# Second attention of a two-block network: float32 value products on the array's column halves, sums on GpSimd

## Chip, cores and metric

One core of one Trainium2 chip. The metric is the device time of one execution in microseconds. Of three runs of the kernel before, the median is 4474.56 us (4474.19 to 4477.1).

## What is computed

Two blocks of a network over 2048 tokens of width 1024, all in float32: block 1 (latent attention, a state space part), block 2 (attention and retention side by side, then routed experts). The change lies in block 2's attention: eight query heads, two key/value heads, 2304 keys (256 of a context and 2048 tokens), head width 64.

```python
def _attend(q, k, v):
    qb = jnp.moveaxis(q.reshape(B, nb, Q_BLOCK, ATTN_KV_HEADS, GQA_GROUP, HEAD_DIM), 1, 0)
    scale = HEAD_DIM ** -0.5
    def one_block(q_blk):
        s = jnp.einsum('bqhgd,bkhd->bhgqk', q_blk, k).astype(jnp.float32) * scale
        p = jax.nn.softmax(s, axis=-1)
        return jnp.einsum('bhgqk,bkhd->bqhgd', p.astype(v.dtype), v)
```

## The kernel before

`whole` runs the phases one after another. `phase_b` projects the tokens; its `do_kv` splits the values into a high and a low part (`R` is the type fp32r, `F` is float32) and stores both. `phase_attn2` (L1310) then runs `Attention2`, with `Retention.steps` in its gaps, and `phase_out2` follows.

`Attention2` works in 32 units: 128 queries of the four heads that share keys, so 512 columns (head, query). A unit goes through 18 key tiles of 128 keys. For a tile t:

- `scores` (L1176): two fp32r products of 512 columns into one PSUM bank `ps`.
- `exps` (L1185): the exponential on ScalarE (L1187) into `p`, and a rounded copy `ph` in fp32r (L1191).
- `rest` (L1193), one tile later: the remainder `pl` = p - ph (L1199), on DVE for even t and on GpSimd (POOL in the rows) for odd t, by the string `LO`. By the string `ACC` the row sums of `ph` are taken by TensorE for ten tiles ("E") and by DVE for eight ("D", L1209, tile `accD`); `fold` splits that sum at the end.
- `values` (L1223), five tiles later (`LAG`): `ph` against both parts of the values (L1232, tile `o`), `pl` against a block of 64 columns of ones beside the high part (L1234, L1238, tile `o1`), and a single row of ones against `ph` and the two parts of the sum (L1236). All are fp32r products of 512 columns, 48 in a unit.

While a unit runs, `top` (L1154) takes the next unit's maxima: 20 products into `pa` (L1161; 16 of 512 columns, four of 256), each with a maximum on DVE (L1162), out of two banks. `finish` (L1240) adds the parts, sends the sums through memory to be spread over partitions, and divides (GpSimd, L1254 and L1265).

Retention takes four steps in a unit (tiles 1, 9, 11, 15, `SIDE`). A chunk of it has six: among them four DVE steps on the state (`rst`, L1049), a power on GpSimd (`r`, L72), four DVE steps that wait for it (`on`, L1076), transposes of `on`, a product on GpSimd (`ot`, L1086), and a spread of queries on GpSimd (`qx`, L966). The last three units have none of it.

Every engine takes its instructions in the order of its own list; the framework's scheduler makes the lists from the order of the code in `run` and adds waits on semaphores.

Of the kernel before, what the change touches and what calls it, by code (L numbers as in the profile page):

```python
# [33 lines left out]
class K:  # L34
    """What every part of the kernel shares: the core, the arguments, constants, small helpers."""
# [76 lines left out]
# Chunks of 16 tokens. Lanes of the tables: (direction, state). A table of powers has 17 entries e:  # L112
# lambda^e forward, lambda^(16 - e) backward.
# [3 lines left out]
def early(k):  # L117
    """What rests on the parameters alone, in small parts."""
# [56 lines left out]
        # Powers 0..16, ascending for both directions: [lanes, e, g].  # L175
# [16 lines left out]
        # Bbar = (lambda_bar - 1) / lambda B  # L192
# [18 lines left out]
        # Tables with e in the direction's order; pw: lambda^s' forward, lambda^(15 - s') backward.  # L211
# [10 lines left out]
        # Bbar with columns (direction, h), zero off its direction.  # L222
# [869 lines left out]
class Attention2:  # L1092
# [92 lines left out]
    def exps(self, u, t):  # L1185
# [4 lines left out]
        if self.HI[t] == "A":  # L1190
            self.nc.scalar.copy(hi, p)  # L1191
# [1287 lines left out]
```

## Time and profile before

| what | value |
|---|---|
| median of three runs | 4474.56 us |
| profiled execution, span of its instructions | 4460.7 us |
| what lies around the span, against the median | 13.9 us |
| TensorE (PE), busy share of the span | 91% |
| DVE | 73% |
| ScalarE (ACT) | 52% |
| GpSimd (POOL) | 45% |

The profile gives the span of its one execution and no device time of its own for it, so the span is set against the median. Busy shares are means over phases with different limits. TensorE's is not a measure of work: its products are pipelined, and a row's duration is the time from its start to its end, which is longer than the step to the next start. In the rows an arrow stands between what is written and what is read, "idle before" is what the engine waited ahead of an instruction, and `x` is a count. A float32 product is two rows, each with half of its passes: `s5_out` asks for 64 products at its L1394 and the trace has 128.

### The profile page before, as it was taken

The numbers are of one execution on the slowest core, as the hardware profiler recorded it, in microseconds if no ns is written. First come the engines' busy times: TensorE is split into PE (matmuls) and PEld (weight loads), VectorE is DVE, ScalarE is ACT, GpSimd is POOL, SyncE is SP. The second block draws the span as 40 slices with busy tenths as digits, with TensorE's granted clock in tenths as the row PEclk, the third lists the DMA queues.
The fourth block names the chain that finished last, engine by engine and source line by source line (L and its number), as shares of the span: only waits on it lengthen the run. The fifth ranks groups of instructions, "written<-read, shape, count | busy, mean of one in ns | idle before, by whom it ended". The sixth has DMA issues, their size and how long they took to land. (4 is left out here: it accounts for less than half of the span.)

```text
span 4460.7 us, 60030 instructions
## 1 busy us (share of the span) xinstructions
PE 4063.1 (91%) x19842; PEld 3214.7 (72%) x19842; DVE 3244.0 (73%) x5326; ACT 2301.0 (52%) x4166; POOL 1988.3 (45%) x2239
## 2 busy tenths in 40 slices
PE   7999889999988989999888888989898799999997
PEld 5777768888876878887666666666587677777775
DVE  7563368887625365534999999999765778888886
ACT  3233455555524343322667777777521556666664
POOL 3430078882003422222555555555300566666664
PEclk9999989999998999999999999999999899999998
DMA  5543852331253464334421111110352788888885
GB/s 142 169 146 109 280 192 74 92 112 53 66 160 123 132 206 127 121 103 135 117 71 52 50 45 43 50 41 25 96 172 95 265 279 280 284 280 275 277 282 184
DMA packets 432999, 647.63 MB, mean 145 GB/s; under 512 B 88576, under 2 KB 228096, under 8 KB 432428
## 3 DMA queue, kind: packets, MB, share of 16 engines
q1 hardware_dynamic: 403868, 562.67, 39.9%
q0 software_dynamic: 21840, 66.25, 4.2%
q10 hardware_dynamic: 6976, 14.85, 1.0%
q8 instruction: 157, 2.57, 0.2%
q14 instruction: 158, 1.29, 0.1%
HBM read 496.33 MB, written 156.10 MB: 146 GB/s over the span
## 5 line engine op out<-in xcount | busy, mean ns | idle before, releaser
L1199 POOL TENSOR_TENSOR pl<-p,ph 128x512 fp32r<-128x512 f32 x288 | 416.1, 1450 | 244.8 <-ACT ph L1191 189.4
L2251 DVE TENSOR_TENSOR wlo<-raw,whi 128x1024 fp32r<-128x1024 f32 x256 | 471.6, 1855 | 66.1 <-ACT whi L2248 66.0
L2248 ACT CAST whi<-raw 128x1024 fp32r<-128x1024 f32 x384 | 394.9, 1048 | 130.9 <-DMA raw<-in_moe_w_up 43.9
L1162 DVE TENSOR_REDUCE nm<-pa 128x1 f32<-128x512 f32 (+1 forms) x640 | 390.0, 623 | 19.7 <-PE pa L1161 18.4
L1187 ACT ACTIVATE p<-ps 128x512 f32<-128x512 f32 x576 | 333.2, 599 | 105.6 <-PE ps L1183 87.0
L1161 PE MATMUL pa<-kk,q 128*128 128x512 f32 (+1 forms) x640 | 266.3, 425 | 95.7 <-DVE nm L1162 85.1
L1191 ACT CAST ph<-p 128x512 fp32r<-128x512 f32 x576 | 342.6, 624 | 7.7
L2251 POOL TENSOR_TENSOR wlo<-raw,whi 128x1024 fp32r<-128x1024 f32 x128 | 319.6, 2504 | 53.5 <-ACT whi L2248 47.4
L310 PE MATMUL z<-wh,hlo 128*128 128x512 f32 (+2 forms) x816 | 304.7, 374 | 0.0
L308 PE MATMUL z<-wh,hhi 128*128 128x512 f32 (+2 forms) x768 | 291.4, 381 | 7.5 <-DVE zo L455 2.4
L309 PE MATMUL z<-wl,hhi 128*128 128x512 f32 (+2 forms) x768 | 289.4, 377 | 2.7 <-DVE wl L319 2.7
L72 POOL TENSOR_TENSOR nr<-nr,mhalf 128x1 f32<-128x1 f32 x98 | 61.7, 631 | 499.2 <-DVE nr L70 441.1
L1199 DVE TENSOR_TENSOR pl<-p,ph 128x512 fp32r<-128x512 f32 x288 | 275.4, 956 | 9.8 <-ACT ph L1191 8.3
L1161 PEld LDWEIGHTS pa<-kk,q 128*128 128x128 f32 x640 | 124.0, 195 | 198.4 <-DVE nm L1162 167.0
L1182 PE MATMUL ps<-q,kk 128*128 128x512 f32 x576 | 241.5, 420 | 0.3
L661 PE MATMUL s<-kn,q 128*128 128x512 f32 x768 | 230.0, 407 | 10.0 <-ACT p L674 5.7
L1238 PE MATMUL o<-pl,v 128*128 128x512 f32 x544 | 220.4, 409 | 17.3 <-DVE pl L1199 12.6
L1232 PE MATMUL o<-ph,v 128*128 128x512 f32 x576 | 233.0, 407 | 2.7 <-DVE oc L1249 2.5
L1183 PE MATMUL ps<-qm,kl 65*128 65x512 f32 x576 | 229.0, 407 | 0.2
L1209 DVE TENSOR_TENSOR accD<-accD,ph 128x512 f32<-128x512 f32 x192 | 224.7, 1170 | 0.3
L693 ACT CAST ph<-pt 128x512 fp32r<-128x512 f32 x256 | 142.8, 596 | 151.1 <-PE pt L65 147.8
L697 DVE TENSOR_TENSOR pl<-pt,ph 128x512 fp32r<-128x512 f32 x256 | 167.9, 685 | 67.4 <-ACT ph L693 66.8
(634 smaller groups left out, 11924.5 us busy)
## 6 DMA issues: line engine op xcount, KB each, us to landing
raw<-in_moe_w_gate SPq DMA_DIRECT2D x128, 512.0 KB
raw<-in_moe_w_up SPq DMA_DIRECT2D x128, 512.0 KB
raw<-in_moe_w_down SPq DMA_DIRECT2D x128, 512.0 KB
raw<-in_w_in SPq DMA_DIRECT2D x136, 256.0 KB
w<-in_w_ada SPq DMA_DIRECT2D x96, 256.0 KB
xt<-in_x SPq DMA_DIRECT2D x32, 512.0 KB
xt<-x SPq DMA_DIRECT2D x28, 512.0 KB
rv<-rv SPq DMA_DIRECT2D x34, 256.0 KB
```

What stands on the lines that cost most here:

```text
L308: nc.tensor.matmul(out, lh, rh, start=start, stop=False)
L309: nc.tensor.matmul(out, lh, rl, start=False, stop=False)
L310: return nc.tensor.matmul(out, ll, rh, start=False, stop=stop)
L1161: nc.tensor.matmul(pa[:, :c1 - c0], q[:, h], kk[:, c0:c1], start=True, stop=True)
L1162: nc.vector.tensor_reduce(nm[:, h, c:c + 1], pa[:, :c1 - c0], axis=AX.X, op=OP.max)
L1182: nc.tensor.matmul(ps, kk[:, ts], q, start=True, stop=False)
L1187: self.nc.scalar.activation(p, u["s"].pop(t), AF.Exp, scale=self.scale)
L1191: self.nc.scalar.copy(hi, p)
L1199: (nc.vector if self.LO[t] == "D" else nc.gpsimd).tensor_tensor(lo, p, hi.bitcast(F), op=OP.subtract)
L1232: nc.tensor.matmul(u["o"], v[:, t, 64:], hi, start=first, stop=last)
L2248: nc.scalar.copy(hi, raw)
L2251: i = eng.tensor_tensor(lo, raw, hi.bitcast(F), op=OP.subtract)
```

## The change

The exponentials are no longer split: `ph`, `pl`, `fold` and the strings are gone. `p` lives in a ring of ten tiles and goes into the products in float32. The values are stored and loaded once, in float32, 64 columns to a tile.

Two key tiles are multiplied together: the even tile's values stand in columns 0 to 63 of the array and give partitions 0 to 63 of `o`, the odd tile's stand in columns 64 to 127 and give partitions 64 to 127. The 512 columns go in two halves of 256, so a pair has four float32 products (column half 0, 1, 0, 1). `finish` adds the two halves of `o` as before, without a third part.

The sums of the exponentials are 17 additions a unit on GpSimd, each onto the result of the last (`acc`), and one float32 product of `acc` with a column of ones at the unit's end. In `do_kv` a copy on ScalarE takes the place of the split.

```diff
 class Attention2:
     LAG = 5
-    RING = 8
+    RING = 10
...
-            v = cp.tile([128, self.NK, 192], R, name=f"v{g}")         # ones, high and low parts
+            v = cp.tile([128, self.NK, 64], F, name=f"v{g}")
...
-            nc.sync.dma_start(v[:, :, 64:].bitcast(F), k.v2[g].rearrange("t p n -> p t n"))
-            nc.gpsimd.tensor_copy(v[:, :, 0:64], k.ones[:, None, 0:64].to_broadcast([128, self.NK, 64]))
+            nc.sync.dma_start(v, k.v2[g].rearrange("t p n -> p t n"))
...
     def exps(self, u, t):
-        p = self.wk.tile([128, 512], F, name="p", bufs=5)
+        u["p"][t] = p = self.wk.tile([128, 512], F, name="p", bufs=self.RING)
         self.nc.scalar.activation(p, u["s"].pop(t), AF.Exp, scale=self.scale)
-        hi = self.wk.tile([128, 512], R, name="ph", bufs=self.RING)
-        u["p"][t] = [p, hi]
-        if self.HI[t] == "A":
-            self.nc.scalar.copy(hi, p)
 
     def rest(self, u, t):
+        if t:
+            acc = u["acc"] if t > 1 else self.wk.tile([128, 512], F, name="acc")
+            self.nc.gpsimd.tensor_tensor(acc, u["acc"], u["p"][t], op=OP.add)
+            u["acc"] = acc
+        else:
+            u["acc"] = u["p"][0]
...
     def values(self, u, t):
         nc = self.nc
...
+        if t % 2 == 0:
+            return
+        if t == 1:
             u["o"] = self.pO.tile([128, 512], F, name="o")
-            u["o1"] = self.pO.tile([128, 512], F, name="o1")
         v = self.kv[u["n"] % 2][2]
-        hi, lo = u["p"].pop(t)
-        nc.tensor.matmul(u["o"], v[:, t, 64:], hi, start=first, stop=last)
...
+        ps = [u["p"].pop(t - 1), u["p"].pop(t)]
+        for half in range(2):
+            cs = slice(256 * half, 256 * half + 256)
+            for i in range(2):
+                nc.tensor.matmul(u["o"][64 * i:64 * i + 64, cs], v[:, t - 1 + i], ps[i][:, cs],
+                                 start=t == 1 and half == 0, stop=t == self.NK - 1 and half == 1)
+        if t == self.NK - 1:
+            u["o1"] = self.pO.tile([1, 512], F, name="o1")
+            nc.tensor.matmul(u["o1"], self.k.ones[:, 0:1], u["acc"], start=True, stop=True)
 
     def finish(self, u):
...
-        nc.scalar.copy(s, o1[64:128])
...
-        nc.gpsimd.tensor_tensor(c, c, s, op=OP.add)
...
         def do_kv(z, s):
...
-            vt = wk.tile([128, 2, 2, 64], R, name="vt")
...
-            split(nc, vt[:, :, 0], vt[:, :, 1], v)
...
+            vt = wk.tile([128, 2, 64], F, name="vt")
+            nc.scalar.copy(vt, v)
```

TensorE's list at the end of a unit, before (`o_25496` is the unit's `o1`; `kk_20808` serves the maxima of the next unit; "waits" names the engine whose semaphore is waited for):

```order
L1161 MATMUL pa<-kk_20808,q 128x512 [waits DVE_49]
L1232 MATMUL o<-ph,v_20810 128x512
L1236 MATMUL o_25496<-ph,on_20802 1x512
L1236 MATMUL o_25496<-sumh,on_20802 1x512
L1182 MATMUL ps<-q,kk_20820 128x512 [waits Activation_49]
L1183 MATMUL ps<-qm,kl_20821 128x512
L1236 MATMUL o_25496<-suml,on_20802 1x512
L1238 MATMUL o_25496<-pl,v_20810 128x512 [waits Pool_49]
L1161 MATMUL pa<-kk_20808,q 128x256 [waits DVE_49]
```

and now (L1155 is `pa`, L1173 and L1174 are the scores, L1201 the value products, L1205 the sums, `o_27650` their tile `o1`):

```order
L1155 MATMUL pa<-kk_20788,q 128x512 [waits DVE_49]
L1173 MATMUL ps<-q,kk_20799 128x512 [waits Activation_49]
L1174 MATMUL ps<-qm,kl_20800 128x512
L1201 MATMUL o<-p,v_20790 64x256 x4
L1205 MATMUL o_27650<-acc,ones 1x512 [waits Pool_49]
L1155 MATMUL pa<-kk_20788,q 128x256 [waits DVE_49]
```

The value products stand in groups of four, and the product of the sums, which waits for GpSimd's last addition, stands right behind the unit's last pair, five tiles into the next unit.

GpSimd's list over about a unit with retention, before:

```order
L966 TENSOR_TENSOR qx<-rq,decays 128x512 [waits PE_49]
L1254 TENSOR_TENSOR oc<-oc,os 64x512 [waits DMAHW4_49,DVE_49,Activation_49]
L1199 TENSOR_TENSOR pl<-p,ph 128x512 [waits Activation_49,Pool_49] x2
L1199 TENSOR_TENSOR pl<-p,ph 128x512 [waits PE_49,Activation_49] x2
L1265 TENSOR_TENSOR oc<-oc,rb 64x512 [waits DMAHW1_49,Pool_49]
L1199 TENSOR_TENSOR pl<-p,ph 128x512 [waits PE_49,Activation_49] x2
L72 TENSOR_TENSOR r_27925<-r_27925,mhalf 128x4 [waits DVE_49]
```

and now (L1184 the additions, L1229 the division):

```order
L1184 TENSOR_TENSOR acc<-p 128x512 [waits Activation_49]
L1184 TENSOR_TENSOR acc<-acc,p 128x512 [waits Activation_49,Pool_49] x8
L966 TENSOR_TENSOR qx<-rq,decays 128x512 [waits DMAHW6_49,PE_49]
L1184 TENSOR_TENSOR acc<-acc,p 128x512 [waits Activation_49,Pool_49] x2
L1229 TENSOR_TENSOR oc<-oc,rb 64x512 [waits DMAHW1_49,DMAHW5_49,DMAHW0_49,DVE_49]
L1184 TENSOR_TENSOR acc<-acc,p 128x512 [waits Activation_49,Pool_49] x5
L72 TENSOR_TENSOR r_27264<-r_27264,mhalf 128x4 [waits DVE_49]
```

Nine subtractions and one addition of a unit have become 17 additions, 16 of which wait for GpSimd's own last one, with retention's instructions between them.

DVE's list around retention's power, before (`r` is made on DVE, raised on GpSimd, and read by `on`):

```order
L70 TENSOR_SCALAR r_25717<-mv 128x4 [waits DVE_49]
L1209 TENSOR_TENSOR accD<-accD,ph 128x512
L1165 TENSOR_REDUCE mx<-nm 128x4 [waits DVE_49]
L1199 TENSOR_TENSOR pl<-p,ph 128x512 [waits Activation_49]
L1076 TENSOR_SCALAR on<-on,mv,r_25717 128x128 [waits Pool_49]
L319 TENSOR_TENSOR suml<-accD,sumh 128x512 [waits Activation_49]
```

and now (L1156 takes the maxima of `pa`):

```order
L70 TENSOR_SCALAR r_24672<-mv 128x4 [waits DVE_49]
L1049 SCALAR_TENSOR_TENSOR rst<-rst,decays,ruf 64x128
L1159 TENSOR_REDUCE mx<-nm 128x4 [waits DVE_49]
L1076 TENSOR_SCALAR on<-on,mv,r_24672 128x128 [waits Pool_49]
L1076 TENSOR_SCALAR on<-on,mv,r_24672 128x128 x3
L1156 TENSOR_REDUCE nm<-pa 128x1 [waits PE_49] x4
```

The subtractions and sums that stood between `r` and `on` are gone, so DVE reaches its wait for GpSimd sooner, with the next maxima behind it.

## Rows read from the trace of the kernel before

**Rows 1.** The page's first line.

```profile
span 4460.7 us, 60030 instructions
```

**Rows 2.** Instructions of tile `ps`: durations min/median/max, first and last start.

```profile
L1182 PE MATMUL ps<-q,kk x576: 387/397/776, 2108.4 to 3185.4; 128*128 128x512 f32 x192
```

**Rows 3.** Windows: busy by engine (instructions), clock, DMA share, GB/s; nine units.

```profile
2466.00:2767.00 301.00, 267.34 (x1188) 187.22 (x1187) 293.47 (x479) 220.06 (x414) 169.73 (x117) 0.97 0.17 46
```

**Rows 4.** Groups on DVE, 2466 to 2767 us: busy us, mean ns, idle before.

```profile
L1162 DVE TENSOR_REDUCE nm<-pa 128x1 f32<-128x512 f32 (+1 forms) x180 | 109.7, 622 | 2.5 <-PE pa L1161 2.3
L1199 DVE TENSOR_TENSOR pl<-p,ph 128x512 fp32r<-128x512 f32 x81 | 76.0, 938 | 2.8 <-ACT ph L1191 2.2
L1209 DVE TENSOR_TENSOR accD<-accD,ph 128x512 f32<-128x512 f32 x54 | 57.9, 1071 | 0.0
L1076 DVE TENSOR_SCALAR on<-on,mv,r 128x128 f32<-128x128 f32 x24 | 20.8, 918 | 0.7 <-POOL r L72 0.7
...
L1209 DVE TENSOR_TENSOR accD<-ph 128x512 f32<-128x512 f32 x9 | 9.1, 1016 | 0.0
L319 DVE TENSOR_TENSOR suml<-accD,sumh 128x512 fp32r<-128x512 f32 x9 | 6.1, 676 | 0.0
```

**Rows 5.** Groups on POOL, 2466 to 2767 us.

```profile
L1199 POOL TENSOR_TENSOR pl<-p,ph 128x512 fp32r<-128x512 f32 x81 | 117.4, 1454 | 67.0 <-ACT ph L1191 47.9 <-PE pa L1161 18.5 <-PE ps L1183 0.6
...
L1265 POOL TENSOR_TENSOR oc<-oc,rb 64x512 f32<-64x512 f32 x9 | 12.8, 1425 | 11.4 <-DMA rb<-a2sum 4.8 <-PE ps L1183 3.8 <-PE pa L1161 1.6
L1086 POOL TENSOR_TENSOR ot<-ot,rg 128x512 f32<-128x512 f32 x6 | 9.7, 1610 | 19.2 <-ACT ot L1084 13.3 <-PE pa L1161 3.2 <-PE o L1238 2.7
L72 POOL TENSOR_TENSOR r<-r,mhalf 128x4 f32<-128x4 f32 x6 | 8.3, 1385 | 25.4 <-DVE r L70 25.4
L966 POOL TENSOR_TENSOR qx<-rq,decays 128x512 f32<-128x512 f32 x6 | 7.9, 1312 | 0.0
```

**Rows 6.** Timeline of PE, 2822 us: start, duration, instruction; fp32r products.

```profile
2822.47 0.40 PE L1232 MATMUL o<-ph,v 128*128 128x512 f32 x1
2822.71 0.39 PE L1236 MATMUL o<-ph,on 128*1 128x512 f32 x1
2822.94 0.40 PE L1238 MATMUL o<-pl,v 128*128 128x512 f32 x1
```

**Rows 7.** Timeline of PE, 1299 us: float32 products of 256 columns.

```profile
1299.70 1.03 PE L1394 MATMUL pz<-tz,ut 128*128 128x256 f32 x4
1300.56 1.03 PE L1396 MATMUL pz<-o,st 128*128 128x256 f32 x4
```

**Rows 8.** Timeline of PE, 324 us: float32 products on 32-column strips of the array.

```profile
324.32 0.18 PE L287 MATMUL pk<-cre,bbr 128*16 128x16 f32 x1
324.33 0.42 PE L284 MATMUL pk<-o_r,bdr 128*32 128x272 f32 x1
324.35 0.18 PE L287 MATMUL pk<-cre,bbr 128*16 128x16 f32 x1
324.38 0.20 PE L287 MATMUL pk<-ncim,bbi 128*16 128x16 f32 x2
324.58 0.39 PE L284 MATMUL pk<-o_r,bdr 128*32 128x272 f32 x1
```

**Rows 9.** Instructions of L1409 (block 1): an addition onto an operand, 128x512.

```profile
L1409 POOL TENSOR_TENSOR sq<-sq x12: 1267/1294/1307, 1425.2 to 1535.6; 128x512 f32<-128x512 f32 x12
```

**Rows 10.** Timeline of POOL, 764 us: the second instruction reads the first's result.

```profile
763.85 0.32 POOL L1369 TENSOR_TENSOR rt<-rt,rt 64x64 f32<-64x64 f32 x1
764.25 1.19 POOL L1370 TENSOR_TENSOR st<-st,rt 64x64 f32<-64x64 f32 x2
```

**Rows 11.** Timeline of POOL, 2624 us.

```profile
2624.83 1.50 POOL L1199 TENSOR_TENSOR pl<-p,ph 128x512 fp32r<-128x512 f32 x1
2626.32 1.27 POOL L1265 TENSOR_TENSOR oc<-oc,rb 64x512 f32<-64x512 f32 x1
2627.55 1.33 POOL L1199 TENSOR_TENSOR pl<-p,ph 128x512 fp32r<-128x512 f32 x1
```

**Rows 12.** Timeline of DVE, 2625 us.

```profile
2625.10 4.12 DVE L1076 TENSOR_SCALAR on<-on,mv,r 128x128 f32<-128x128 f32 x4
```

More of the change, by code (lines that the diff above doesn't have):

```diff
@@ L1101 @@
     END = 9
-    HI = "AAAAAAAAAAAAAAAAAA"
-    LO = "DPDPDPDPDPDPDPDPDP"
-    ACC = "EDEDEDEDEDEDEDEDEE"
-    ROW = "A"
     def __init__(self, k, ctx, scale):
@@ L1120, in __init__ @@
         self.kv = []
-        self.ones = cp.tile([128, 1], R, name="on1")
-        nc.vector.tensor_copy(self.ones, k.ones[:, 0:1])
         self.q = {0: self.load_q(0)}
@@ L1169, in top @@
             self.k.tr(pt[0:1, h], mx[:, h:h + 1])
-        if self.ROW == "D":
-            nc.vector.tensor_scalar(qm[64:65], pt[0:1], -1.0, None, op0=OP.mult)
-        else:
-            nc.scalar.mul(qm[64:65], pt[0:1], -1.0)
+        nc.scalar.mul(qm[64:65], pt[0:1], -1.0)
         yield
@@ L1198, in rest @@
-        lo = self.wk.tile([128, 512], R, name="pl", bufs=self.RING)
-        (nc.vector if self.LO[t] == "D" else nc.gpsimd).tensor_tensor(lo, p, hi.bitcast(F), op=OP.subtract)
-        u["p"][t] = hi, lo
-        e = self.ACC[t]
-        if e in "DP":
-            eng = nc.vector if e == "D" else nc.gpsimd
-            had = u["acc"].get(e)
-            if had is None:
-                u["acc"][e] = hi.bitcast(F), False
-            else:
-                acc = had[0] if had[1] else self.wk.tile([128, 512], F, name="acc" + e, bufs=1)
-                eng.tensor_tensor(acc, had[0], hi.bitcast(F), op=OP.add)
-                u["acc"][e] = acc, True
-            if t == max(self.ACC.rfind(x) for x in "DP"):
-                self.fold(u)
@@ L1214, in fold @@
-    def fold(self, u):
-        nc = self.nc
-        accs = [x[0] for x in u["acc"].values()]
-        for x in accs[1:]:
-            nc.vector.tensor_tensor(accs[0], accs[0], x, op=OP.add)
-        u["sum"] = [self.wk.tile([128, 512], R, name="sum" + n, bufs=1) for n in "hl"]
-        split(nc, *u["sum"], accs[0])
+        if t:
[4 more added lines that the diff above has]
+            u["acc"] = u["p"][0]
@@ L1223, in values @@
     def values(self, u, t):
         nc = self.nc
-        first, last = t == 0, t == self.NK - 1
-        if first:
+        if t % 2 == 0:
+            return
+        if t == 1:
             u["o"] = self.pO.tile([128, 512], F, name="o")
-            u["o1"] = self.pO.tile([128, 512], F, name="o1")
         v = self.kv[u["n"] % 2][2]
-        hi, lo = u["p"].pop(t)
-        nc.tensor.matmul(u["o"], v[:, t, 64:], hi, start=first, stop=last)
-        if first:
-            nc.tensor.matmul(u["o1"], v[:, t, 0:128], lo, start=True, stop=False)
@@ L1235, in values @@
-        for x in ([hi] if self.ACC[t] == "E" else []) + (u["sum"] if last and "sum" in u else []):
-            nc.tensor.matmul(u["o1"][0:1], self.ones, x, start=False, stop=False)
-        if not first:
-            nc.tensor.matmul(u["o1"], v[:, t, 0:128], lo, start=False, stop=last)
+        ps = [u["p"].pop(t - 1), u["p"].pop(t)]
[4 more added lines that the diff above has]
+                                 start=t == 1 and half == 0, stop=t == self.NK - 1 and half == 1)
@@ L1244, in finish @@
         c = wk.tile([64, 512], F, name="oc")
-        s = wk.tile([64, 512], F, name="os", bufs=1)
         w = wk.tile([1, 512], F, name="ow", bufs=1)
@@ L1278, in run @@
                 if t == 0:
-                    us[n] = dict(n=n, p={}, s={}, acc={})
+                    us[n] = dict(n=n, p={}, s={})
                     for _ in ahead:
@@ L1634, in phase_b @@
     k.k2 = k.scratch("k2", [2, 2, 128, NK * 128])
-    k.v2 = k.scratch("v2", [2, NK, 128, 128])
+    k.v2 = k.scratch("v2", [2, NK, 128, 64])
     k.rq = k.scratch("rq", [NT, 128, 256])
@@ L1715, in do_kv @@
             kt = (s + 2) % (NT + 2)
-            vt = wk.tile([128, 2, 2, 64], R, name="vt")
             v = z[:, 128:256].rearrange("p (n c) -> p n c", c=64)
-            split(nc, vt[:, :, 0], vt[:, :, 1], v)
-            nc.sync.dma_start(k.v2[:, kt].rearrange("h p n -> p h n"), vt.bitcast(F).rearrange("p h a n -> p h (a n)"))
+            vt = wk.tile([128, 2, 64], F, name="vt")
+            nc.scalar.copy(vt, v)
+            nc.sync.dma_start(k.v2[:, kt].rearrange("h p n -> p h n"), vt)
             def late():
```

4 lines of the change are left out of this document (removed).

## Prediction

> **What bounds the kernel now.** I went from the page to the tile of the scores, then to a stretch, then to single instructions. The execution spans 4460.7 us [rows 1]. The scores of the second attention's 576 key tiles start from 2108.4 to 3185.4 us [rows 2], so 32 units fill a quarter of the span, some 33 us each, and nothing outside this stretch changes by more than a few us. I worked on the window from 2466 to 2767 us: DVE takes 180 maxima in it, twenty for each unit [rows 4], so it is nine units of 33.4 us. In it DVE is busy for 293.5 of 301 us, ScalarE for 220.1, GpSimd for 169.7 [rows 3]. TensorE's 267.3 there is no bound: its rows overlap, and its true work is counted below. DVE idles 7.5 us in nine units, and TensorE's waits for `pa` are waits for DVE. So DVE sets the pace, with maxima of 109.7 us, subtractions of 76.0, sums of 57.9 and 9.1 and the split of the sum, 6.1 [rows 4].
>
> **What the change removes.** From DVE: 76.0 + 57.9 + 9.1 + 6.1 = 149.1 us of nine units, which leaves 144.4, or 16 us a unit. ScalarE loses 18 casts a unit and two smaller copies, and gains nothing; it had slack already. The values' split in the projections goes (18 tiles, each at most the 0.68 us of the split's row [rows 4], 12 us if nothing covered it); TensorE's products cover it, so I count 0. The loads and stores of the values halve and stand behind the keys' loads; also 0. If that cover were gone, both together would be the 12 us, a gain. So DVE is not late next; GpSimd or TensorE is.
>
> **GpSimd, worked out.** The additions are new in this place. The nearest row is block 1's addition of the same size onto its operand: 1.29 us with little spread [rows 9]. Two instructions that don't depend on each other overlap by 0.04 us on GpSimd (1.27 us long, the next one 1.23 after it [rows 11]); one that reads the last one's result starts 0.08 us after its end [rows 10]. An addition in the chain so takes 1.37 us, the first of a unit 1.25. Nine units: 144 x 1.37 = 197.3, and 9 x 1.25 = 11.3, and nine divisions at 1.25, 11.3. Retention's six chunks: `ot` and `qx` six times each at 1.25 us, 15.0 (their means of 1.61 and 1.31 hold waits for DVE), and `r` 8.3 [rows 5]. Sum 243.2.
>
> Something is to be added for DVE's small steps. Four `on` steps took 4.12 us together, one to each GpSimd instruction [rows 12], while GpSimd went through its instructions 1.49, 1.23 and 1.33 us apart [rows 11]: DVE waits for GpSimd, and GpSimd loses about 0.1 us each time. For the 24 `on` steps and the 24 `rst` steps that is 4.8 us. Sum 248, **27.6 us a unit**. The ends for an addition: 1.25 us if the wait on its own result costs nothing, which gives 25.6 us a unit; 1.45 us as the subtractions take beside today's DVE [rows 5], plus 0.08, which gives 30.4. I take the value near the low end, since DVE's two-operand work of 512 columns, which runs beside these subtractions now, is what goes.
>
> The Trainium skill speaks against this step: "GPSIMD Engine Reference", section "Engine selection", puts elementwise additions on VectorE, GpSimd being about twice as slow with two inputs. The rows agree on the ratio (0.68 against 1.29 us). By that rule the 17 additions on DVE would make 16 + 17 x 0.68 = 27.6 us a unit there, before any of the waits that lifted today's sums to 1.07 us: no better here than GpSimd, which otherwise is idle.
>
> **TensorE, worked out.** Products in fp32r of 512 columns start 0.23 us apart, the row of ones included [rows 6]: the 128x32 strip that it uses costs no gap when the next product takes the whole array. A unit has 36 for scores, 16 and four half ones for maxima, and 48 for values and sums: 12.6 + 11.2 us. Transposes and retention's products are about 3 (an estimate: some 28 rows a unit at half of the float32 row below). Together 26.8 of 33.4. A float32 row of 256 columns steps by 0.86 / 4 = 0.215 us [rows 7], and each product is two rows. A pair of key tiles has eight rows: 1.72 us if they go one after another, 0.86 if the column halves run at the same time. These are the ends, and the trace shows which is nearer. Block 1 has float32 products on two 32-column strips. A product of the second strip starts at 324.33, between the two rows of a product of the first strip (324.32 and 324.35), and two more of the first start at 324.38, while its own next row comes 0.25 us later [rows 8]. So strips run together, and a later strip is taken ahead. I take 0.86. Values: 9 x 0.86 = 7.7; the product of the sums, two rows of 512 columns, 0.86. TensorE: 12.6 + 3 + 8.6 = **24.2 us a unit**, 2.6 less than now.
>
> **The sum.** GpSimd at 27.6 us is the longest list, TensorE at 24.2 and DVE at 16 plus its waits for GpSimd (at most 48 x 1.3 us in nine units, 7 a unit) stay below. Today's bound idles 2.5%; GpSimd's instructions wait for more (`r`, `ot` and the division waited 25.4, 19.2 and 11.4 us in nine units [rows 5], most of it because GpSimd was ahead), so I add 4%: 28.7 us a unit against 33.4, a gain of 4.7. For the first unit, which waits for loads, nothing; for 31 units 146 us. The span becomes 4315 us. The median stands 13.9 us above this span; with the same 14 around it the time is **4329 us**.
>
> The queues: TensorE's product of the sums waits for the last addition, with the next unit's products behind it. The addition can start when the tile's exponential is there, four tiles earlier, some 6 us, so only a GpSimd that lags by more holds TensorE. That is how its pace reaches the others. SP's queue holds fewer bytes and no new step.
>
> **Rivals.**
> *The halves don't run together.* The change then does not do what it says: rows 8 show a narrow product of 16 columns beside a long one, not two long ones. A pair costs 1.72 us, values 15.5, TensorE 12.6 + 3 + 15.5 + 0.9 = 32.0 us a unit, and with 2 us of waits 34.0, over DVE's 33.4 today. It decides from about 1.65 us a pair. 31 x 0.6 = 19 us: 4494 us, slower. Against it stands that TensorE took a later strip ahead at all. Chance 0.13.
>
> *In-order starts.* The second half's first row waits until both rows of the first half's product have started; a pair then takes five steps, 1.08 us, TensorE 26.2 us a unit. That is near GpSimd's 27.6, two lists that hold each other up more: 29.4 us a unit, 31 x 4.0 = 124, 4351 us. Rows 8 speak against it. The Trainium skill, "TensorE: Matmul & The Clock Gate", section "Part 3: Packing small matmuls — row/col tiling", has matmuls start strictly in program order; by that rule, this is the case, and the trace differs, since the later product's start lies between the earlier one's two rows. Chance 0.15.
>
> *DVE stands in line.* In DVE's list `on` now comes two or three instructions after `r`, and waits for GpSimd's power (1.39 us [rows 5]) behind whatever additions are queued; then four steps take 4.1 us [rows 12]. The maxima stand behind, `pa` has two banks, and TensorE stops. With two additions queued that is 2.7 + 1.4 + 4.1 us a chunk, of which two free banks cover some three tiles, 4.8; 3.4 us a chunk, two chunks in three units, is 2.3 us a unit: 31.0, 31 x 2.4 = 74, 4400 us. For it: TensorE's waits for `pa` today. Against it: when TensorE stops, GpSimd's queue empties, and the wait with it. Chance 0.16.
>
> **How the numbers follow.** Forecast 0.56, and the three rivals 0.15, 0.16 and 0.13. A measurement of this kernel can tell about 0.2%, 9 us. The low end: additions without the wait, 25.6 x 1.04 = 26.6 us a unit, 31 x 6.8 = 211, or 4264; I stop at 4268, since retention's share is not that free. The high end takes in the third rival and the dearer additions (30.4 x 1.04 = 31.6 us, 31 x 1.8 = 56, 4419), which I cut to 4412, since half of what beside DVE made the subtractions dear is gone. Left out is the first rival and a few per cent on both sides. The first three cases are faster, less a little for stalls that eat all: 0.85. The first rival gives slower 0.11 and, with that rest, no change 0.04.
>
> **What would show it.** Right: the scores' tiles span some 31 x 4.7 us less; in a middle stretch GpSimd is busy over 90% with additions of 1.3 us, 1.37 apart; the four value products of a pair start within some 0.7 us, halves two by two; DVE falls below 80%; what follows the attention keeps its length. Wrong: value rows 0.215 us apart one by one, and units of 33 us or more with TensorE as the bound; additions of 1.5 us or more; TensorE waiting at the product of the sums or at `pa` for more than 3 us a unit; or a gain that comes back as waits after the attention.

## The result, and the profile after

The changed kernel takes 4431.42 us (median of four runs, 4424.64 to 4436.68) where the kernel before takes 4475.83 beside it: a ratio of 0.9895 (95% interval 0.9881 to 0.9909), 44 us faster. The forecast was 4329 us in a range from 4268 to 4412. The direction was right, two thirds of the gain did not come, and the time lies outside the range.

The first two lines of the page, and the page's groups that are new or answer to [rows 4, 5]:

```profile
span 4433.4 us, 60786 instructions
...
PE 4092.9 (92%) x20674; PEld 3107.4 (70%) x20674; DVE 2779.5 (63%) x4763; ACT 1966.4 (44%) x3526; POOL 2202.0 (50%) x2461
...
L1184 POOL TENSOR_TENSOR acc<-acc,p 128x512 f32<-128x512 f32 x512 | 660.1, 1289 | 168.4 <-ACT p L1178 141.2
L1156 DVE TENSOR_REDUCE nm<-pa 128x1 f32<-128x512 f32 (+1 forms) x640 | 394.0, 633 | 334.3 <-PE pa L1155 331.8
...
L1201 PE MATMUL o<-p,v 128*64 128x256 f32 x2304 | 380.0, 404 | 0.0
...
L1201 PEld LDWEIGHTS o<-p,v 128*64 128x64 f32 x2304 | 157.0, 139 | 175.1 <-issue 125.4
```

The additions take 1.29 us, as forecast. But GpSimd waits for exponentials (141.2 us), DVE's maxima for products (331.8 us), and TensorE's loads of the value tiles wait 125.4 us for nothing that the profile names. The one maximum `mx` per unit marks the units (instructions of tile `mx`; of after, then of before):

```profile
L1159 DVE TENSOR_REDUCE mx<-nm x32: 155/174/176, 2135.6 to 3135.3; 128x4 f32<-128x20 f32 x32
```

```profile
L1165 DVE TENSOR_REDUCE mx<-nm x32: 154/160/175, 2124.9 to 3161.5; 128x4 f32<-128x20 f32 x32
```

Thirty-one units last 999.7 us, or 32.2 each, where they lasted 1036.6, or 33.4; the forecast was 28.7. The rest of the execution went from 3424 to 3434 us, which says little: in the profiled executions of the runs below it lies between 3409 and 3452. So the miss lies in the units. Four of them (windows, columns as in [rows 3]):

```profile
2495.00:2532.40 37.40, 32.57 (x170) 18.71 (x168) 23.15 (x44) 14.13 (x26) 27.34 (x23) 0.91 0.12 32
2532.40:2561.70 29.30, 29.30 (x163) 17.49 (x161) 16.00 (x30) 13.29 (x24) 24.37 (x20) 1.00 0.25 62
2561.70:2590.60 28.90, 28.90 (x147) 15.68 (x146) 16.66 (x36) 14.64 (x28) 23.33 (x20) 1.00 0.22 57
2590.60:2629.60 39.00, 34.17 (x170) 19.61 (x169) 23.31 (x44) 14.13 (x26) 28.01 (x23) 0.87 0.11 32
```

The windows' ends lie up to 1 us beside the units': by the starts of `mx` these four last 36.4, 31.2, 28.1 and 37.9 us. There are two kinds. In the second and third TensorE (first column of busy time) never stops: they are TensorE's, at 29.7 us on the mean in place of 24.2. The first and the last are 7 to 8 us longer than that mean, with TensorE idle for 4.8 us and a lower granted clock; from the sixth unit on every third is so.

**A slow unit, close up.** The timelines of DVE, POOL and PE at 2516 us:

```profile
2516.46 2.52 DVE L70 TENSOR_SCALAR r<-mv 128x4 f32<-128x4 f32 x1
2518.89 0.68 DVE L1156 TENSOR_REDUCE nm<-pa 128x1 f32<-128x512 f32 x1
2520.11 4.10 DVE L1076 TENSOR_SCALAR on<-on,mv,r 128x128 f32<-128x128 f32 x4 [0.54 <-POOL r L72]
2524.13 1.01 DVE L1156 TENSOR_REDUCE nm<-pa 128x1 f32<-128x256 f32 x2
```

```profile
2516.45 1.27 POOL L1229 TENSOR_TENSOR oc<-oc,rb 64x512 f32<-64x512 f32 x1
2517.68 1.26 POOL L1184 TENSOR_TENSOR acc<-acc,p 128x512 f32<-128x512 f32 x1
2519.05 1.02 POOL L72 TENSOR_TENSOR r<-r,mhalf 128x4 f32<-128x4 f32 x1
2520.04 4.09 POOL L1184 TENSOR_TENSOR acc<-acc,p 128x512 f32<-128x512 f32 x3
```

```profile
2520.66 0.40 PE L1174 MATMUL ps<-qm,kl 65*128 65x512 f32 x1
2524.60 0.80 PE L1155 MATMUL pa<-kk,q 128*128 128x512 f32 x1 [3.54 <-DVE nm L1156]
2525.32 1.12 PE L1201 MATMUL o<-p,v 128*64 128x256 f32 x4
```

DVE's `r`, four columns, lasts as long as two instructions of GpSimd; four `on` steps last as long as three additions that stood queued, 4.10 beside 4.09 us. The maxima stand behind them, both `pa` banks are full, and TensorE stops for 3.54 us. Then it runs slower: the granted clock is 0.62 from 2520 to 2525 us and 0.78 from 2525 to 2532, that is partly the 1.2 GHz level, and the four value rows take 1.12 us, against 0.65 at the 2.4 GHz level below.

**An ordinary unit, close up.** Timeline of PE:

```profile
2566.55 0.38 PE L1201 MATMUL o<-p,v 128*64 128x256 f32 x1
2566.86 0.50 PE L1173 MATMUL ps<-q,kk 128*128 128x512 f32 x1
2567.20 0.40 PE L1174 MATMUL ps<-qm,kl 65*128 65x512 f32 x1
2567.53 0.65 PE L1201 MATMUL o<-p,v 128*64 128x256 f32 x4
2568.11 0.50 PE L1155 MATMUL pa<-kk,q 128*128 128x512 f32 x1
2568.45 0.39 PE L1173 MATMUL ps<-q,kk 128*128 128x512 f32 x1
2568.68 0.40 PE L1174 MATMUL ps<-qm,kl 65*128 65x512 f32 x1
```

Products on the whole array step by 0.23 us (2568.45 to 2568.68). Before the value rows the step is 0.33 (2567.20 to 2567.53), after the last of them 0.31 in place of 0.215 (2566.55 to 2566.86), and the row that follows a group takes 0.34 (2568.11 to 2568.45). So the change to narrow tiles and back costs some 0.1 us at each of three steps. The first line is the second row of a lone product: the scheduler has split the groups, 387 in TensorE's list where 288 are written, 12.1 a unit in place of 9.

### The profile page after: what moved, and what is told of

Read it like the earlier page. It is cut to its first block, busy times and chain, and to the rows that moved or that the text cites. A ratio compares the mean times of both kernels' runs of the same rounds, so it can differ in the third digit from the quotient of the medians.

```text
span 4433.4 us, 60786 instructions
## 1 busy us (share of the span) xinstructions
PE 4092.9 (92%) x20674; PEld 3107.4 (70%) x20674; DVE 2779.5 (63%) x4763; ACT 1966.4 (44%) x3526; POOL 2202.0 (50%) x2461
## 5 line engine op out<-in xcount | busy, mean ns | idle before, releaser
L1184 POOL TENSOR_TENSOR acc<-acc,p 128x512 f32<-128x512 f32 x512 | 660.1, 1289 | 168.4 <-ACT p L1178 141.2
L1156 DVE TENSOR_REDUCE nm<-pa 128x1 f32<-128x512 f32 (+1 forms) x640 | 394.0, 633 | 334.3 <-PE pa L1155 331.8
L1201 PE MATMUL o<-p,v 128*64 128x256 f32 x2304 | 380.0, 404 | 0.0
L1155 PE MATMUL pa<-kk,q 128*128 128x512 f32 (+1 forms) x640 | 269.9, 451 | 49.5 <-DVE nm L1156 44.2
L1201 PEld LDWEIGHTS o<-p,v 128*64 128x64 f32 x2304 | 157.0, 139 | 175.1 <-issue 125.4
L1155 PEld LDWEIGHTS pa<-kk,q 128*128 128x128 f32 x640 | 116.9, 195 | 209.2 <-DVE nm L1156 96.8
L1173 PE MATMUL ps<-q,kk 128*128 128x512 f32 x576 | 245.4, 426 | 0.3 <-ACT p L1178 0.3
L1174 PE MATMUL ps<-qm,kl 65*128 65x512 f32 x576 | 230.7, 405 | 0.0
L739 PE MATMUL o<-ph,v 128*128 128x256 f32 x1024 | 216.8, 293 | 0.2 <-ACT ph L693 0.2
L1445 POOL TENSOR_TENSOR y<-v,gt 128x512 f32<-128x512 f32 x16 | 21.6, 1347 | 350.3 <-DVE v L1441 350.3
L674 ACT ACTIVATE p<-s,nm 128x512 f32<-128x512 f32 x256 | 177.3, 708 | 8.5 <-DVE s L666 8.1
```

The source lines that it names most:

```text
L1155: nc.tensor.matmul(pa[:, :c1 - c0], q[:, h], kk[:, c0:c1], start=True, stop=True)
L1156: nc.vector.tensor_reduce(nm[:, h, c:c + 1], pa[:, :c1 - c0], axis=AX.X, op=OP.max)
L1173: nc.tensor.matmul(ps, kk[:, ts], q, start=True, stop=False)
L1174: nc.tensor.matmul(ps, kl[:, ts], qm, start=False, stop=True)
L1184: self.nc.gpsimd.tensor_tensor(acc, u["acc"], u["p"][t], op=OP.add)
L1201: nc.tensor.matmul(u["o"][64 * i:64 * i + 64, cs], v[:, t - 1 + i], ps[i][:, cs], start=t == 1 and half == 0, stop=t == self.NK - 1 and ha ...
```

## Theories and runs

**Theory.** (1) GpSimd's additions hold up DVE's steps of retention (`r`, `on`, `rst`), the maxima behind them, and so TensorE, whose clock then falls. (2) TensorE's list is longer than 24.2 us by what changes of tiling cost, and so is the bound. **Rivals:** the slow units come of TensorE's or DVE's order, whoever adds; the steps at a group's ends are waits; the halves gain little.

"Unit" is the time from the first to the last `mx` over 31; the clock is that of 2466 to 2767 us. Both are of the one profiled execution, "us" is the median of all. A ratio is to the kernel before on the same chip.

| run | us | ratio (interval) | unit | clock |
|---|---|---|---|---|
| after | 4431.4 | 0.9895 (0.9881, 0.9909) | 32.2 | 0.96 |
| e1_on_scalar | 4385.5 | 0.9807 (0.9790, 0.9823) | 30.7 | 1.00 |
| e3_pe_order | 4430.3 | 0.9911 (0.9894, 0.9927) | 31.7 | 0.95 |
| e2_sums_dve | 4367.2 | 0.9772 (0.9756, 0.9788) | 30.1 | 0.99 |
| e13_idle_gpsimd | 4687.3 | one run | 40.2 | 0.86 |
| e7_whole_array | 4550.3 | one run | 35.7 | 0.97 |
| e5_half_order | 4370.4 | one run | 30.1 | 0.99 |
| e11_half_groups | 4414.3 | one run | 32.1 | 0.99 |
| e4_quads | 4346.3 | 0.9735 (0.9714, 0.9755) | 29.7 | 0.99 |
| e6_scalar_order | 4411.0 | 0.9867 (0.9851, 0.9884) | 31.4 | 0.94 |
| e12_quads_free | 4450.9 | 0.9957 (0.9939, 0.9974) | 33.2 | 0.90 |
| e9_sixes | 4369.6 | 0.9794 (0.9762, 0.9826) | 30.0 | 0.98 |
| e10_quads_scalar | 4400.8 | 0.9843 (0.9824, 0.9863) | 31.4 | 0.95 |
| e14_early_queries | 4349.6 | 0.9721 (0.9692, 0.9750) | 29.2 | 0.99 |
| e15_early_gpsimd | 4412.5 | 0.9864 (0.9835, 0.9893) | 31.1 | 0.95 |

### e1: `on` on ScalarE

```diff
+            nr = wk.tile([128, HR], F, name="nr")
+            nc.gpsimd.tensor_tensor(nr, mv[:, :, 0], r4, op=OP.mult)
+            nc.scalar.mul(nr, nr, -1.0)
...
-                nc.vector.tensor_scalar(on[:, h], on[:, h], mv[:, h, 0:1], r4[:, h:h + 1], op0=OP.subtract, op1=OP.mult)
+                nc.scalar.activation(on[:, h], on[:, h], AF.Identity, scale=r4[:, h:h + 1], bias=nr[:, h:h + 1])
```

> Retention's normalisation `on` goes from VectorE to ScalarE (its bias from one small product on GpSimd), so no VectorE instruction waits for GpSimd's power any more; all else stays. In the changed kernel units of the second attention last 29.0 us, but every third some 37.5 to 39. Theory (the maxima stand in VectorE's list behind `on`): the slow units fall to 31 or less, some ten units by 7 us each, 70 us: 4360 us (4340 to 4385), and the granted clock stays at 1.00 in them. Rival (the slow units come from GpSimd's or TensorE's own queue, `on` only stands where the wait shows): units of 36 us and more stay, 4420 to 4445.

Measured: 4385.5 us, 46 under the changed kernel. Windows of three units:

```profile
2536.50:2565.20 28.70, 28.23 (x144) 15.20 (x140) 13.81 (x26) 15.88 (x32) 23.15 (x20) 1.00 0.21 56
2565.20:2596.70 31.50, 29.95 (x163) 17.55 (x163) 18.91 (x38) 15.26 (x30) 25.41 (x22) 1.00 0.14 39
2596.70:2628.00 31.30, 31.30 (x173) 18.43 (x173) 17.18 (x40) 14.48 (x26) 26.92 (x23) 1.00 0.23 60
```

The slow unit is gone, and the clock stays at 1.00. The time lies just above the range. By `mx`, the slow units, 36.2 to 37.9 us in the changed kernel's middle, fell to 31.5, not further; those of 31.2 us stayed, and the short ones grew from 28.2 to 28.7. Sign and place are as theory 1 has them. What is left, 30.7 us a unit, is TensorE's: busy 295.21 of 301 us.

### e3: TensorE's products in the written order

```diff
+    def mm(self, *a, **kw):
+        with self.k.tc.issue_after(self.pe.ins) if self.pe else ExitStack():
+            self.pe = self.nc.tensor.matmul(*a, **kw)
```

All products of the second attention but transposes and retention's go through `mm`, which ties each to the one before, so that the scheduler keeps the written order.

> TensorE's products of the second attention keep the order in which they are written, so that the four products of a pair of key tiles stay together: 9 groups a unit in place of 12.1; no work changes. Theory (each change of the array's tiling costs about 0.2 us in and out, and a product that was split off runs without its partner): an ordinary unit goes from 29.0 to 27.3 to 28.2 us, 25 to 55 us in all: 4376 to 4406; the slow third units stay. Rival A (the gaps at the groups' ends are waits that move elsewhere): units of 29.0, 4425 to 4437. Rival B (a fixed order puts products behind ones that wait): gaps on TensorE of over 1 us before scores, 4440 or more.

Measured: 4430.3 us, nothing gained; ordinary units of 30.2 us, slow ones of 35. The groups are nine, and the mean unit of the profiled execution is 0.5 us shorter, but that execution is the fastest of the four (4415.6 us). The fixed list waits elsewhere; in the changed kernel TensorE waits here for `nm` alone, 14.5 us (waits of PE, 2466 to 2767 us, in total, times and longest):

```profile
PE pt L65 <- DVE on L1076: 7.8, 7, 2.0
PE pa L1138 <- DVE nm L1161: 5.9, 5, 2.5
PE pt L65 <- DVE mx L1164: 2.7, 3, 0.9
```

The time is that of rival A, the waits are of rival B's kind, though at `pt` and `pa`, not at scores. This run does not price a change of tiling; the next serve as pairs in this fixed order.

### e2: the additions on VectorE (on e3)

```diff
-            self.nc.gpsimd.tensor_tensor(acc, u["acc"], u["p"][t], op=OP.add)
+            self.nc.vector.tensor_tensor(acc, u["acc"], u["p"][t], op=OP.add)
```

> With the written order of TensorE's products (as in the run beside it), and the additions of the exponentials on VectorE in place of GpSimd. Theory (the slow units come of GpSimd's additions: VectorE's small steps wait one addition each, and the power stands behind additions): `on` takes under 0.5 us a step, the units are even, and VectorE is the bound at 16 + 17 x 0.68 = 27.6 us and its waits, 28 to 30 us a unit: 4320 to 4385. Rival (it is the place of `on` in VectorE's list, whoever adds): every third unit still lasts 36 us or more and the time is within 15 us of the run beside it. Rival B (two-operand sums on VectorE slow down beside other work, as today's sums did at 1.07 us): 16 + 18 = 34 us a unit, 4480 or more.

Measured: 4367.2 us, 63 less than e3 by one line, and even units of 29.7. The same DVE groups of after (first) and of e2, 2466 to 2767 us:

```profile
L1076 DVE TENSOR_SCALAR on<-on,mv,r 128x128 f32<-128x128 f32 x28 | 20.5, 792 | 5.0 <-POOL r L72 5.0
```

```profile
L1189 DVE TENSOR_TENSOR acc<-acc,p 128x512 f32<-128x512 f32 x162 | 120.8, 746 | 2.4
...
L1076 DVE TENSOR_SCALAR on<-on,mv,r 128x128 f32<-128x128 f32 x28 | 8.3, 338 | 2.5 <-POOL r L72 2.5
```

`on` still waits for GpSimd's power, but takes 338 ns in place of 792 (616 in e3). The additions now stand in DVE's list, so the list is not the same; against the rival of the list's order the next run speaks, which keeps the list of e2 in this stretch.

### e13: GpSimd adds besides, and nobody reads it (on e2)

```diff
+            idle = self.wk.tile([128, 512], F, name="idle")
+            self.nc.gpsimd.tensor_tensor(idle, u["p"][t - 1], u["p"][t], op=OP.add)
```

> On the run with the additions on VectorE and TensorE's written order (4367 us, even units of 29.7 us): GpSimd makes an addition of the same size per key tile besides, of two exponentials into a tile that nothing reads. Every engine's order but GpSimd's stays, and no other engine needs its result (the exponentials' buffers come free after it). Theory (GpSimd's additions hold up VectorE's two-operand instructions while both run): VectorE's `rst`, `on` and `r` steps and its own additions take 1.0 us or more each in place of 0.2 to 0.7, VectorE becomes the bound at 33 us a unit or more: 4450 or more, with TensorE waiting for `nm`. Rival (what held up VectorE was only the wait for GpSimd's results, the power behind its queue): within 20 us of 4367.

Measured: 4687.3 us, 320 over e2, units of 40.2 us. DVE groups, 2466 to 2767 us:

```profile
L1189 DVE TENSOR_TENSOR acc<-acc,p 128x512 f32<-128x512 f32 x119 | 133.6, 1123 | 1.6
...
L70 DVE TENSOR_SCALAR r<-mv 128x4 f32<-128x4 f32 x5 | 10.8, 2164 | 0.0
...
L1070 DVE BATCH_NORM_STATS2 bs<-on 128x6 f32<-128x128 f32 x24 | 5.2, 273 | 0.0
```

DVE's addition goes from 746 ns in e2 to 1123, `rst` from 336 to 577, `on` from 338 to 480, and `r`, which reads one tile of four columns, from 157 to 2164. The normalisation's sums stay (278 ns in e2, 273 here), and so do the maxima (683 and 680) and the product `sm`, which reads two tiles, one of them in PSUM (678 and 667). So it is not the number of operands that tells the two kinds apart. DVE waits for GpSimd's power for 1.7 us of 301, so the rival, that wait, is out. The work on GpSimd alone slows DVE; theory 1 is shown. The 320 us are more than its price: ScalarE also waits 12.8 us of 301 for the additions that nobody reads, since the exponentials' buffers come free behind them, and the granted clock is 0.86.

### e7: the value products on the whole array (on e3)

```diff
-                self.mm(u["o"][64 * i:64 * i + 64, cs], v[:, t - 1 + i], ps[i][:, cs],
-                        start=t == 1 and half == 0, stop=t == self.NK - 1 and half == 1)
+                self.mm(u["o"][:, cs], v[:, t - 1 + i], ps[i][:, cs],
+                        start=t == 1 and half == 0 and i == 0, stop=t == self.NK - 1 and half == 1 and i == 1)
```

> With the written order of TensorE's products: the value products use the whole array (the values doubled to 128 columns, so the second key tile is added to the first on the same rows and the final sum of two halves adds a copy of itself: the output is another). No column tiling is left, so no change of tiling in the stretch, and the two key tiles go one after another: 1.72 us a pair in place of 0.86, without some 0.2 us at each group's ends. Theory (the halves run together and a change of tiling costs 0.2 us a group): TensorE takes 9 x (0.86 - 0.2) = 5.9 us more a unit than the run with column halves in the same order, 33 to 34.5 us for ordinary units, and 100 to 185 us more in all. Rival (halves gain little, or changes cost 0.5 us and more): at most 40 us more.

Measured: 4550.3 us, 120 over e3, inside the range; 4.0 us a unit, where 5.9 was expected. One group in the timeline of PE of this run, then one of e2, whose list has the same order:

```profile
2593.52 0.40 PE L1139 MATMUL ps<-qm,kl 65*128 65x512 f32 x1
2593.75 1.89 PE L1139 MATMUL o<-p,v 128*128 128x256 f32 x8
2595.29 0.47 PE L1139 MATMUL pa<-kk,q 128*128 128x256 f32 x1
2595.60 0.39 PE L1139 MATMUL ps<-q,kk 128*128 128x512 f32 x1
2595.83 0.39 PE L1139 MATMUL ps<-qm,kl 65*128 65x512 f32 x1
```

```profile
2601.52 0.40 PE L1138 MATMUL ps<-qm,kl 65*128 65x512 f32 x1
2601.85 1.08 PE L1138 MATMUL o<-p,v 128*64 128x256 f32 x8
2602.87 0.62 PE L1138 MATMUL pa<-kk,q 128*128 128x256 f32 x2
2603.32 0.40 PE L1138 MATMUL ps<-q,kk 128*128 128x512 f32 x1
```

(The `x2` of the last fence are a product of 256 and one of 512 columns.) From the row ahead to the row right behind the pair would read 1.77 against 1.35, but on the whole array the last of its rows falls into the next step, 0.31 us. So I read on to the third row behind: with one product of 256 and one of 512 columns in between, it is 2.31 us on the whole array and 1.80 on the halves. The halves run together, but a pair gains 0.51 us, not 0.86; the steps at the group's ends take back the rest. Both groups are float32, and the step ahead of the group is 0.23 us here and 0.33 on the halves, so that gap comes with the halves and not with the type.

### e5: first, first, second, second (on e2)

```diff
-        for half in range(2):
-            cs = slice(256 * half, 256 * half + 256)
-            for i in range(2):
+        for i in range(2):
+            for half in range(2):
+                cs = slice(256 * half, 256 * half + 256)
```

> On the run with the additions on VectorE and TensorE's written order (4367 us): in a pair, both column blocks of the first key tile come before both of the second, so that the products on the two column halves no longer alternate in the program (first, first, second, second). No work changes. Theory A (TensorE looks one product ahead): one of the three steps has both halves, a pair takes 1.29 us in place of 0.86, 3.9 us a unit, 120 us: 4470 to 4500. Theory B (it looks further, so the order within a pair does not matter): 4355 to 4380. Theory C (nothing runs together unless the rows alternate): 0.86 us a pair more, 7.7 us a unit, 240 us: 4600.

Measured: 4370.4 us, as e2. Theory B: TensorE takes a product of the other half from behind two of the first; in the trace the rows still start in twos, 13 ns apart (2593.787 and 2593.800 us).

### e11 and e4: seventeen and five groups a unit (on e2)

Of e11, where the two column blocks of a pair stand apart, and of e4, with four key tiles to a group:

```diff
+        b = t - 1 if t % 2 else t - 2
+        for half in ([0, 1] if t == self.NK - 1 else [0] if t % 2 else [1]):
```

```diff
-        if t % 2 == 0:
+        if t % 4 != 3 and t != self.NK - 1:
             return
...
+        for b in range(t // 4 * 4, t, 2):
```

> On the run with the additions on VectorE and TensorE's written order (9 groups a unit of 29.7 us, 4367 us): the two column blocks of a pair stand apart, one after an odd key tile's scores and one after the next even tile's, so 17 groups a unit of one column block each; the two key tiles still alternate in each. Same products, twelve buffers for the exponentials in place of ten. Theory (0.29 us a group for the change of tiling): 8 x 0.29 = 2.3 us a unit, 72 us: 4440 (4425 to 4455), TensorE busy the whole unit. Rival (the gaps at the ends of a group are waits for other engines): 4360 to 4385.

> On the run with the additions on VectorE and TensorE's written order (units of 29.7 us, 4367 us): the value products of four key tiles in one group, so 5 groups a unit in place of 9; twelve buffers for the exponentials in place of ten. No work changes. Theory (a group's way into the narrow tiling and out of it costs 0.10 us before its first row, 0.10 after its last and 0.10 in the row that follows, 0.29 together): 4 x 0.29 = 1.2 us a unit, 36 us in all: 4331 (4318 to 4345), units of 28.5 us. Rival (the gap is a wait for weights or for a buffer that comes back elsewhere, or the longer group of 1.7 us makes ScalarE and VectorE wait): units of 29.4 us or more, 4355 or more.

Measured: 4414.3 and 4346.3 us, with e2's 4367.2 between. Both moved the way of the theory, and by less; neither is in its range, and the units of e4, 29.7 us, are the rival's. 47 us for eight groups more is 0.19 us a group (47 / 31 / 8), 21 for four fewer 0.17. By the units of the profiled executions the two steps are 0.26 and 0.08, so each by itself is rough; e11 and e4, both with twelve buffers, differ by 0.18 (times) and 0.20 (units). In e4 DVE is busy 278.17 of 301 us, so it is late next; in e11 TensorE is busy 295.48. So a group costs about 0.19 us in the time, below the 0.29 that I read off single steps.

### e15 and e14: the additions alone, with some of TensorE's waits taken out (on e4)

```diff
-    TOP = (1, 1, 1, 1, 2, 1, 1, 1, 2, 1, 1, 1, 2, 1, 1, 1, 1, 1)
+    TOP = (1, 1, 2, 1, 1, 2, 1, 1, 2, 1, 1, 2, 1, 1, 2, 1, 1, 1)
...
-        self.q = {0: self.load_q(0)}
+        self.q = {i: self.load_q(i) for i in range(2)}
```

> On the run with groups of four key tiles (additions on VectorE, written order, 4346 us): the queries of a unit are loaded one unit sooner (three buffers), and the maxima's steps come up to two tiles sooner in a unit, so that the transposes of the maxima stand behind other products. In that run TensorE waited some 1 us at them in each unit (row starts 0.97 to 1.14 us apart), up to 0.95 us for the queries, and each third unit had 3.4 us at half clock. Theory (TensorE's waits, with the clock that falls after them, and not VectorE's 92% set the 29.7 us): 28.3 to 28.9 us a unit, 25 to 45 us: 4300 to 4321. Rival (VectorE is the bound): 29.4 us or more a unit, 4335 or more.

> The same kernel with the additions back on GpSimd, one line. TensorE's order, groups and loads are those of the run beside it. Theory (the additions on GpSimd hold up VectorE's small steps `r`, `on` and `rst`, the maxima behind them and so TensorE, whose clock then falls): two or three units in three are even with those of the run beside it, a third one is 4 to 8 us longer, 2 us a unit on the mean: 40 to 90 us over the run beside it. Rival (the lock costs nothing once TensorE's list has room for it): within 15 us, or faster, since VectorE is freed.

Measured: 4349.6 us for e14, no better than e4, so its theory failed: TensorE's waits at `pt`, 13.5 us of 301 in e4, are gone, and those at `pa` rose from 1.7 to 12.3. Its unit is 0.6 us shorter; the profiled executions differ by 32 us outside the units (span less units: 3448 against 3416), and why was not settled. The line that puts the additions back on GpSimd costs 63 us: 4412.5, with a clock of 0.95. All three kinds of units are longer, not one in three: 29.0, 32.3 and 34.5 us in the middle, where e14 has 27.1, 27.8 and 31.2. With the same order of products, groups and loads, that is theory 1 alone, the second time at 63 us. Waits of PE in e15, 2466 to 2767 us:

```profile
PE pa L1138 <- DVE nm L1161: 19.0, 6, 5.2
PE pt L65 <- DVE on L1076: 10.3, 3, 3.4
```

### Four runs that missed: e6, e12, e9, e10

They combine the edits above: e6 is e1 with e3; e12 is e1 with groups of four in free order; e9 is e2 with e1 and groups of six; e10 is e4 with e1.

```diff
-        if t % 2 == 0:
+        if t % 6 != 5:
             return
```

> `on` on ScalarE (4386 us alone, even units of 30.7 us) together with TensorE's written order; the additions stay on GpSimd. Theory (the written order saves 3.1 groups a unit at 0.29 us once the slow units are gone): 0.9 us a unit, 28 us: 4358 (4345 to 4372). Rival (the waits that a written order brings cost as much as the groups it saves, as in the run of the order alone, where the sum was 1 us): 4378 to 4395.

> `on` on ScalarE, the additions on GpSimd, no fixed order (4386 us, even units of 30.7 us, TensorE busy 295 of 301 us): the value products written in groups of four key tiles, which the scheduler leaves as 8.7 groups a unit in place of 12.2. Theory (TensorE bounds this kernel, 0.29 us a group): 3.5 x 0.29 = 1.0 us a unit, 31 us: 4355 (4340 to 4368). Rival (GpSimd, busy 250 of 301 us, and the waits for it bound the unit): 4378 to 4395.

> Additions on VectorE, `on` on ScalarE, TensorE's written order and six key tiles in a group: 3 groups a unit; fourteen buffers for the exponentials. Theory (0.29 us a group, TensorE the bound): 6 x 0.29 = 1.7 us a unit under the 29.7 us of nine groups, 28.0 us a unit, 54 us: 4313 (4300 to 4335). Rival A (VectorE, 27.3 us busy a unit, becomes the bound with its waits): 28.7 us or more, 4330 to 4345. Rival B (a group of 2.6 us holds up the scores, with two banks each for scores and maxima): 29.5 us or more, 4360 or more.

> The run with groups of four key tiles (additions on VectorE, written order, 4346 us) with `on` on ScalarE as well. VectorE was busy 278 of 301 us there (92%), TensorE 282. Theory (VectorE is the bound now, and what leaves it shortens the unit): `on` is 24 to 28 steps of some 0.3 us in ten units, 0.8 us a unit, 25 us: 4322 (4310 to 4338). Rival (the two lists hold each other up at 29.7 us whatever leaves VectorE, since the order of TensorE's products is fixed): 4340 to 4355.

Measured: 4411.0, 4450.9, 4369.6 and 4400.8 us. e6 and e12 are slower than e1 and e10 slower than e4, against every expectation; e9 lies where its rival B had it. Timeline of DVE in e6, where retention's state steps now stand one behind another beside the additions:

```profile
2595.22 4.86 DVE L1049 SCALAR_TENSOR_TENSOR rst<-rst,decays,ruf 64x128 f32<-64x128 f32 x3 [0.20 <-PE pt L1061]
```

Three steps, of 0.34 us each in e2, last 4.86 us, and TensorE stops for 2.51 us at `pa`; so `on` was one of the held-up steps, not the only one. In e12 and e10 TensorE waits elsewhere (timeline of PE, e12 and then e10; last, of ScalarE's waits in e12, 2466 to 2767 us, the one for GpSimd: in total, times and longest):

```profile
2570.57 0.60 PE L65 MATMUL pt<-ident,mx 128*1 128x128 f32 x4 [1.97 <-DVE mx L1162]
2572.56 0.80 PE L1176 MATMUL ps<-q,kk 128*128 128x512 f32 x1 [1.40 <-ACT p L1181]
```

```profile
2628.45 1.24 PE L65 MATMUL pt<-ident,on 128*128 128x128 f32 x3 [1.85 <-ACT on L1079]
```

```profile
ACT nr L1076 <- POOL nr L1075: 31.4, 6, 5.5
```

With `on` on ScalarE the wait for GpSimd has moved there: ScalarE stands up to 5.5 us at `nr`, the small product behind GpSimd's power, with the exponentials behind it in its list. It is 12.0 us of 301 in e1, 16.9 in e6, 11.2 in e10 and 31.4 in e12; that it makes e12's 65 us was not shown. Beside these stops the granted clock is lower: in the window it is 0.90 in e12 and 0.95 in e10, where e1 has 1.00. What a stop costs by itself and what the clock adds was not separated. For e9 I know only that neither TensorE (278.88 of 301 us) nor DVE (264.51) is full, and that ScalarE waits no longer for scores than in e4 (100.0 and 108.0 us), so rival B's reason is not shown.

## Why the prediction was wrong

Two steps failed: TensorE's sum of 24.2 us a unit, whose list fills 30.5 in e1, and the argument by which DVE's wait behind GpSimd was left out of the forecast, worth 1.5 to 2.0 us a unit. GpSimd, the forecast's bound, never was one.

- **What bounds the kernel before, and what DVE sheds:** right. DVE fell to 175 of 301 us and waits for TensorE; that is 18.8 us a unit where I had 16, with the steps that GpSimd stretches in it.
- **GpSimd, 27.6 us a unit:** right in its price, wrong as the bound. Queued additions start 1.35 to 1.36 us apart (2509.91, 2511.26 and 2512.62 us; 1.37 forecast) and 1.38 to 1.44 beside the four `on` steps, but GpSimd is busy 23 to 24 us in ordinary units and waits for exponentials.
- **The step on the Trainium skill's rule:** wrong. By "GPSIMD Engine Reference", section "Engine selection", elementwise additions belong on VectorE; I worked out 27.6 us there and called it no better, since GpSimd was otherwise idle. Two pairs of runs that differ in this line give 63 us for VectorE, both in the fixed order; the changed kernel with this line alone was not run. My sum compared the engines' lists and left out what GpSimd's additions do to DVE's.
- **The halves run together, 0.86 us a pair:** right in kind. Strips do run at once, and not only in program order (e5), so the rival of in-order starts is out, and the one of halves that do not run together too (e7). What a pair gains is 0.51 us, with the group's ends, and not 0.86.
- **TensorE, 24.2 us a unit: this term failed.** "The 128x32 strip that it uses costs no gap" carried the row of ones [rows 6] over to value tiles on half of the columns, and the splitting of the groups was not counted. From each row's start to the next row's, waits included, TensorE's list fills 30.5 us a unit in three units of e1 (2536.5 to 2628.0 us): scores and maxima 16.0 (forecast 12.6), values 10.7 (7.7), small products 2.8 (3), the sums 0.95 (0.86). That is 6.3 more, of which 4.5 would have been hidden below GpSimd's 28.7. By the price from e11, 12.1 groups make 2.3 us of it; split-off products without a partner and waits share the rest, and I have no run that parts them. The Trainium skill has the rule that I should have weighed: "TensorEngine Tiling (Array Packing)", section "Key Properties", says that a change of the tiling mode drains the engine. The steps of 0.31 to 0.34 us agree; the row of ones, which steps by 0.23 us [rows 6], shows no such cost.
- **"DVE stands in line" (0.16, 31.0 us a unit):** the mechanism was right, and my argument against it wrong: "when TensorE stops, GpSimd's queue empties, and the wait with it". The exponentials were there ahead, three additions stood queued at 2520 us, and the queue emptied only after the four steps were through. The Trainium skill's "SBUF — State Buffer", section "SBUF: two separate sides", calls the port pair of DVE and GpSimd an exclusive lock for a whole instruction; 4.10 beside 4.09 us agrees. e13 shows the hold-up; that a port is its cause no run here shows.
- **The range:** it took the cases one at a time. Two came together: TensorE's longer list (30.7 us a unit in e1, 2.0 over the forecast) and the slow units (1.5 more in the changed kernel; 2.0 by the pairs with 63 us). 3.5 us over 31 units is 109 us; the miss is 102.
- **Two readings:** the 13.9 us do not lie around the span. The changed kernel's profiled execution took 4435.2 us with a span of 4433.4, so 1.8 us lie around it, and the profiled execution of the kernel before must have been some 12 us faster than the median. The forecast holds without it, as the median before less 146 us. And of GpSimd's steps "1.49, 1.23 and 1.33 us apart" the last is a duration [rows 11], which weighs little in 27.6 us.

## What to carry to other kernels

An engine that is idle is not free: before work goes to GpSimd, look for the DVE instructions that will run beside it (here sums of tiles in SBUF and steps on one such tile with scalars were held up, maxima and `bs` were not), and for what stands behind them in DVE's list. Where products change between tilings of the array, count the changes in the list that the scheduler makes, price each, and put as many products into a group as the next engine bears. The additions on VectorE with groups of four key tiles (e4) take 4346 us, less than both kernels: 0.9735 of the kernel before (0.9714 to 0.9755).

## What was not expected of the hardware

- GpSimd's additions stretch even the smallest DVE step: `r`, four columns, took 2.52 us at 2516.46, and 0.15 in e6 with GpSimd idle:

```profile
2601.65 0.15 DVE L70 TENSOR_SCALAR r<-mv 128x4 f32<-128x4 f32 x1
```

- A pair of float32 products on column halves takes 0.51 us less than on the whole array, not half of 1.72. A group's change of tiling and back costs about 0.19 us in the time.
- TensorE's order can be made better and the kernel slower. e12 has 8.7 groups a unit where e1 has 12.1, and takes 65 us more, with more stops and a clock of 0.90 against 1.00.
